# Low parts of 30 weights: from a VectorE subtraction to a ScalarE negative and an adding DMA

## The chip, the cores and the metric

One core of one Trainium2 chip runs the whole program. The metric is the device time of one execution in microseconds (us); lower is better. Engines are named as the profile names them: PE (matmuls), PEld (weight loads of PE), DVE (VectorE), ACT (ScalarE), POOL (GpSimd), SP (SyncE, which issues most transfers). Each engine runs its own instructions in order, and semaphores make it wait for others.

## What is computed

One layer over 1024 latent tokens of width 1024, with 256 context tokens:

```python
rgx, gate, s5u = split(modulate(x) @ w_in)        # three times 1024 columns
xc = centred_dwconv(rgx)                          # width 4
r, i = sigmoid(block_diag(xc)), sigmoid(...)      # 8 heads, both directions
h = linear_scan(exp(log_a), sqrt(-expm1(2 log_a)) * (i * xc))
rg = (h_fwd + h_bwd) * gelu(gate)
y = s5_fwd(s5u) + s5_bwd(s5u) + d * s5u           # complex diagonal states
s5 = gelu(y) * sigmoid(gelu(y) @ glu)
x = layer_norm(alpha * x + g1 * (concat(rg, s5) @ w_out))
x = layer_norm(alpha * x + g2 * sq_relu_mlp(modulate(x)))
```

Matmuls keep float32 accuracy by splitting both operands in a high part, rounded to the PE's fp32r format, and a low part, the rest: a product is wh·xh + wh·xl + wl·xh.

## The kernel before

**Weights.** `weights(src)` loads a 128x1024 block of a weight (512 KB) into a slot `wr` (three of them) by SP, and `split` makes two tiles of it: `wh`, a cast by ACT (line 98), and `wl = wr - wh`, a subtraction by DVE (`tt`, line 47). There are three slots each for `wh` and `wl`. `wr` is free when both have read it.

**Stages.** `project(m, ...)` multiplies one block of `w_in` with the tokens (line 380, products `ps_mm`). Its 24 blocks are eight for the RG-LRU input (`proj_rgx`, the first two of which take another way into the same sums), eight for the S5 input (`proj_s5`) and eight gates (`proj_gate`). While the S5 blocks and the S5 matrices are worked on, `rg_head` runs eight heads one after the other, each a chain: convolution on DVE, cast `xch` on ACT (line 421), gate products on PE (line 435, `ps_g`), sigmoids on ACT (line 437), after a table load exponentials (lines 442 and 443), after another the square root (line 446, tile `rr`), and then on DVE a step on `rr`, products and the linear scans (lines 455 to 458).

`s5_in` makes the S5 states' inputs H on PE and copies them out of PSUM (lines 603 to 606; for the second half all on ACT). `scan` runs 127 steps of three small DVE operations (tiles sT, sU, H) for each half of the groups; the two halves are interleaved. `proj_gate` evicts with a Gelu (line 636, tile `ge`) and multiplies by the RG-LRU's result on DVE.

The RG-LRU's half of the output projection has eight column blocks m. `mix_in(k)` loads the mixed rows k and splits them (tile `mh`): for k 0 to 4 the low part is a negative by ACT (line 664) and a DMA issued by POOL that adds the source from memory (line 665), for k 5 to 7 a subtraction by DVE. Columns 0 and 1 go together over all k (`k_outer`, line 694), columns 2 to 5 one by one (`prod`, line 675) through two PSUM banks with the tag "mm", columns 6 and 7 together again. `put_part` copies each bank out by ACT (line 681, tile `pt`).

`s5_states` copies the scanned states in the order in which the S5 output reads them (`h`, lines 724 and 725; for the first half both by ACT, 128 partitions in two halves), and `s5_out` multiplies them (lines 751 to 753, `ps_so`) and takes a Gelu (line 754, `gs`).

**Order.** The program is written stage by stage, but a list scheduler with its own estimates of durations and due times sets the order of each engine's queue. So an edit to one helper can move instructions far from it. A queue's order is fixed when the program is built.

Of the kernel before, what the change touches and what calls it, by code (L numbers as in the profile page):

```python
# [8 lines left out]
F32R = mybir.dt.float32r  # L9
I32 = mybir.dt.int32  # L10
AF = mybir.ActivationFunctionType
# [4 lines left out]
P = 128  # L16
# [25 lines left out]
def build(nc, tc, a, out):  # L42
    V, S, G, PE = nc.vector, nc.scalar, nc.gpsimd, nc.tensor
    MUL, ADD, SUB, MAX = ALU.mult, ALU.add, ALU.subtract, ALU.max

    def tt(o, x, y, op, eng=None):
        (eng or V).tensor_tensor(out=o, in0=x, in1=y, op=op)  # L47
# [10 lines left out]
    def ld(o, i):  # L58
        return nc.sync.dma_start(out=o, in_=i)

    def after(ins):
        return nullcontext() if ins is None else tc.issue_after(ins.ins)
# [4 lines left out]
    def f(t):  # L67
        return t.bitcast(F32)
# [3 lines left out]
    def pool(name, bufs=1, side="left", space=None, stack=es):  # L72
        kw = dict(name=name, bufs=bufs)
        if space is not None:
            kw["space"] = space
        else:
            kw["side"] = side
            kw["reuse_waits"] = "tile"
        return stack.enter_context(tc.tile_pool(**kw))
# [11 lines left out]
    wp = pool("wp")  # L91
# [3 lines left out]
    def split(raw, n, tag, hb, lb=None):  # L95
        hi = wp.tile([P, n], F32R, tag=tag + "h", name=tag + "h", bufs=hb)
        lo = wp.tile([P, n], F32R, tag=tag + "l", name=tag + "l", bufs=lb or hb)
        S.copy(hi, raw)  # L98
        tt(lo, raw, f(hi), SUB)
        return hi, lo  # L100
# [5 lines left out]
        S.activation(t, f(h), AF.Identity, bias=bias, scale=-1.0)  # L106
        stt(lo, x, scale, t, MUL, ADD)

    def weights(src, behind=None):
        raw = wp.tile([P, 1024], F32, tag="wr", name="wr", bufs=3)  # L110
        with after(behind):
            ld(raw, src)
        return split(raw, 1024, "w", 3)


    cols = con.tile([P, row(NCOLS)], F32, name="cols")
# [66 lines left out]
    def tmp(w=64, dt=F32):  # L183
        cnt[0] += 1
        return pp.tile([P, row(w)], dt, name=f"t{cnt[0]}")[:, 0:w]
# [25 lines left out]
    k = tmp()  # L211
# [85 lines left out]
    def fin_mod(mc, k, src):  # L297
        tt(mc, src, adab[:, :, k:k + 1].to_broadcast([P, 2, 2]), ADD)
        ts(mc[:, 1, :], mc[:, 1, :], 1.0, ADD)

    wrg = [weights(a["w_in"][m]) for m in range(2)]
    early = []
    for m in range(2):
# [3 lines left out]
    for k in range(KT):  # L307
# [18 lines left out]
        for r, src, pl_, n in ((0, xr, xlp, NL), (1, xc, xcp, NC)):  # L326
            h = pl_.tile([P, n], F32R, name=f"x{r}h{k}")
            lo = pl_.tile([P, n], F32R, name=f"x{r}l{k}")
            t = sup.tile([P, n], F32, tag=f"xt{r}", name="xt", bufs=1)
# [15 lines left out]
        for m in range(2):  # L345
            wh, wl = wrg[m]
# [20 lines left out]
    alt = [0]  # L367

    def project(m, ctx, evict, behind=None, load=None):
        wh, wl = weights(a["w_in"][m], load)  # L370
        src = [([x[:, s] for x in xh], [x[:, s] for x in xl], 512) for s in HS] + [(ch_, cl_, NC)]
        for i in (2, 0, 1) if ctx else (0, 1):
            hs, ls, n = src[i]
            alt[0] ^= ctx
            ps = psx.tile([P, n], F32, tag="si" if alt[0] and ctx else "mm", name="ps_mm", bufs=2)
            for k in range(KT):
                ks = slice(k * P, (k + 1) * P)
                with after(None if k else behind):
                    for c, (w, x) in enumerate(((wh, hs[k]), (wh, ls[k]), (wl, hs[k]))):
                        PE.matmul(ps, w[:, ks], x, start=(k == 0 and c == 0), stop=(k == KT - 1 and c == 2))  # L380
            evict(i, ps)
# [9 lines left out]
    def proj_rgx(m):  # L391
        xr = rp.tile([P, row(RGW)], F32, tag="rx", name="rx", bufs=2)
        for z in (slice(0, 1), slice(257, 260), slice(1284, 1286)):
            G.memset(xr[:, z], 0.0)

        def evict(i, ps):
            o, n = ((260, 512), (772, 512), (1, NC))[i]
            S.copy(xr[:, o:o + n], ps)

        if m < 2:  # L400
            for i, ps in enumerate(early[m]):
                evict(i, ps)
        else:
            project(m, True, evict)
        return xr
# [67 lines left out]
    def proj_s5(m):  # L473
        us = ev.tile([P, T8, NCH], F32, tag="us", name="us", bufs=1)

        def evict(i, ps):
            if i < 2:
                S.copy(us[:, :, CC + i::2], ps.rearrange("p (t c) -> p t c", t=T8))
            else:
                S.copy(us[:, :, 0:CC], ps.rearrange("p (c t) -> p t c", t=T8))  # L480

        project(16 + m, True, evict)
        d = dr.tile([T8, P, NCH], F32, name=f"u{m}")
        st_(d.rearrange("t p c -> p t c"), us)
        uscr[m] = d
# [184 lines left out]
    def prod(ps, w, x, js):  # L670
        (wh, wl), c = w, 0
        for k in range(KT):
            ks = slice(k * P, (k + 1) * P)
            for u, v in ((wh, x[k][:, 0]), (wh, x[k][:, 1]), (wl, x[k][:, 0])):
                PE.matmul(ps, u[:, ks], v[:, js], start=(c == 0), stop=(c == 3 * KT - 1))  # L675
                c += 1

    def put_part(m, pss):
        t = sc.tile([P, NL], F32, tag="gs", name="pt", bufs=2)
        for j, ps in enumerate(pss):  # L680
            S.copy(t[:, HS[j]], ps)
        part[m] = dr.tile([P, NL], F32, name=f"pt{m}")
        (G.dma_start if m > 5 else S.dma_start)(out=part[m], in_=t)

    def k_outer(ws, xs, tags, name, ks_=range(KT)):

        pss = [[psx.tile([P, 512], F32, tag=t, name=name, bufs=2) for j in range(2)] for t in tags]
        for i, k in enumerate(ks_):
            x = xs(k)
            ks = slice(k * P, (k + 1) * P)  # L690
            for (wh, wl), pp_ in zip(ws, pss):
                for j, ps in enumerate(pp_):
                    for c, (u, v) in enumerate(((wh, x[:, 0]), (wh, x[:, 1]), (wl, x[:, 0]))):
                        PE.matmul(ps, u[:, ks], v[:, HS[j]], start=(i == 0 and c == 0), stop=(i == KT - 1 and c == 2))
        return pss

    mix = []
# [2 lines left out]
        mix.append(mix_in(k))  # L700
        return mix[k]

    for m, pss in enumerate(k_outer([weights(a["w_out"][0, m]) for m in range(2)], mix_next, ("rg", "si"), "ps_wo")):
        put_part(m, pss)
    for m in range(2, 6):
        w = weights(a["w_out"][0, m])
        pss = []
        for j in range(2):
            pss.append(psx.tile([P, 512], F32, tag="mm", name="ps_wo", bufs=2))
            prod(pss[j], w, mix, HS[j])  # L710
        put_part(m, pss)
    for m, pss in enumerate(k_outer([weights(a["w_out"][0, m]) for m in (6, 7)], lambda k: mix[k], ("rg", "mm"), "ps_wo",
                                    (3, 4, 5, 6, 7, 0, 1, 2))):
        put_part(6 + m, pss)
    mixst.close()
# [87 lines left out]
    mxs, mix = {}, []  # L803
# [23 lines left out]
    for m in range(8):  # L827
        if m > 1:
            if m + 2 < 8:
                ahead.append(weights(a["glu"][m + 2]))  # L830
            w = ahead.pop(0)
# [148 lines left out]
    for j in range(2):  # L980
        ys = []
        for m in range(8):
            if 8 * j + m + 2 < 16:
                ahead.append(weights(a["w_out"][1, (m + 2) % 8]))
            w = ahead.pop(0)
# [86 lines left out]
    for p in range(0, NP1 + 4, 2):  # L1072
        if p < NP1:
            raw = wp.tile([P, 1024], F32, tag="wr", name="wr", bufs=3)
# [4 lines left out]
        wh, wl = w_ahead.pop(0)  # L1079
        for e in range(2):  # L1080
# [3 lines left out]
            t = ap_.tile([P, 512], F32, tag="r", name="p2", bufs=4)  # L1084
# [55 lines left out]
    def combo_next():  # L1140
        while len(c_ahead) < 4 and c_n[0] < len(stream):
            c = c_n[0]
            c_n[0] += 1
            if c % 2 == 0:
                c_tile[0] = [wp.tile([P, 1024], F32R, tag=t, name=t, bufs=3) for t in ("wh", "wl")]
            n, p = stream[c]
            src_ = operand(n, p)
            hi, lo = (x[:, HS[c % 2]] for x in c_tile[0])
            S.copy(hi, src_)  # L1149
            tt(lo, src_, f(hi), SUB)  # L1150
            c_ahead.append((hi, lo))
        return c_ahead.pop(0)

    XS = {"1": x0[0::2], "5": xt_[0], "6": xt_[1], "7": xt_[2], "3": x1, "4": xt_[3]}
    def rt():
        return ap_.tile([P, 512], F32, tag="r", name="r", bufs=4)
# [5 lines left out]
    for n, p in stream:  # L1162
        w = combo_next()
# [3 lines left out]
        if n == "1":  # L1167
# [3 lines left out]
            v, t = p2t.pop(p), rt()  # L1171
# [273 lines left out]
def program(arrays):  # L1445
    import concourse.bacc as bacc

    nc = bacc.Bacc("TRN2", target_bir_lowering=False, num_devices=1, dynamic_dma_scratch_size=1024)
    aps = {n: nc.dram_tensor(f"in_{n}", v.shape, mybir.dt.from_np(v.dtype), kind="ExternalInput").ap() for n, v in arrays.items()}
    out = nc.dram_tensor("out_0", (D, NL), F32, kind="ExternalOutput").ap()  # L1450
    with tile.TileContext(nc) as tc:
        build(nc, tc, aps, out)
    return nc
# [10 lines left out]
```

## Time and profile before

| | us |
|---|---|
| median of 3 runs | 1596.51 (1595.15 to 1600.73) |
| the profiled execution | 1594.69 |
| its span | 1592.9 |
| PE busy | 1476.7 (93%) |
| DVE busy | 1256.8 (79%) |
| ACT busy | 843.0 (53%) |
| POOL busy | 71.0 (4%) |
| mean granted clock of PE | 0.974 |

The span is what the trace covers. Busy shares are means over stages with different limits, so the table alone doesn't tell what an operation costs. A row of the timeline has the start, the duration, the engine, the line, the operation with output <- input, how many such stand in a row, and in brackets how long the engine had been idle and what ended that. Starts of pipelined instructions lie closer than their durations.

### The profile page before, as it was taken

How to read it: one execution, taken by the hardware profiler on the slowest of the kernel's cores; microseconds unless marked ns; L12 is line 12 of the kernel's file. 1: busy time of each engine (PE TensorE's matmuls, PEld its weight loads, DVE VectorE, ACT ScalarE, POOL GpSimd, SP SyncE). 2: the span in 40 equal slices, each digit the busy share in tenths (PEclk: the TensorE clock that was granted, in tenths of full speed). 3: DMA queues.
4: the chain of work that ended last, by engine and by line, in shares of the span. 5: the costliest groups of instructions: out<-in, count | busy, mean ns of one | idle time of the engine just before them, and what ended most of it. 6: DMA issues, size and time to landing. Idle time of an engine off the chain costs nothing. (4 is left out here: it accounts for less than half of the span.)

```text
span 1592.9 us, 20440 instructions
## 1 busy us (share of the span) xinstructions
PE 1476.7 (93%) x7148; PEld 1202.4 (75%) x7148; DVE 1256.8 (79%) x2555; ACT 843.0 (53%) x1178; POOL 71.0 (4%) x141
## 2 busy tenths in 40 slices
PE   7899998999978999699999799989899899999997
PEld 2687777778756878598878677867788788888886
DVE  7899999998866989635978789778787566667877
ACT  4675656666795331954233576444555554344425
POOL 0000000000000000000000011111111000000000
PEclk9999999999999999799999999999999999999999
DMA  7623323323664752983768576777764786776703
GB/s 255 233 94 119 115 99 120 105 106 119 231 215 137 209 183 91 264 201 119 228 207 265 173 242 232 279 248 268 245 219 167 268 287 215 263 251 210 240 7 106
DMA packets 131382, 304.16 MB, mean 191 GB/s; under 512 B 16208, under 2 KB 47440, under 8 KB 129872
## 3 DMA queue, kind: packets, MB, share of 16 engines
q1 hardware_dynamic: 104048, 237.45, 46.9%
q0 software_dynamic: 13184, 47.72, 8.4%
q10 hardware_dynamic: 14048, 17.70, 3.1%
q8 instruction: 56, 0.92, 0.2%
q14 instruction: 46, 0.38, 0.1%
HBM read 219.52 MB, written 83.30 MB: 190 GB/s over the span
## 5 line engine op out<-in xcount | busy, mean ns | idle before, releaser
L98 ACT CAST wh<-wr 128x1024 fp32r<-128x1024 f32 x113 | 118.4, 1051 | 230.0 <-PE ps_m L1276 73.8
L47 DVE TENSOR_TENSOR wl<-wr,wh 128x1024 fp32r<-128x1024 f32 (+1 forms) x161 | 170.5, 1060 | 83.7 <-ACT wh L98 77.2
L1066 PE MATMUL ps_m<-xt,wh 128*128 128x512 f32 x512 | 160.7, 395 | 0.0
L1276 PE MATMUL ps_m<-bh,wh 128*128 128x512 f32 x392 | 153.7, 392 | 3.8 <-ACT bh L1238 3.7
L1276 PE MATMUL ps_m<-bl,wh 128*128 128x512 f32 x392 | 153.4, 391 | 0.5 <-DVE bl L47 0.5
L1276 PE MATMUL ps_m<-bh,wl 128*128 128x512 f32 x392 | 153.3, 391 | 0.0
L380 PE MATMUL ps_mm<-x0h,wh 128*128 128x512 f32 x352 | 140.3, 399 | 1.0 <-ACT wh L98 1.0
L380 PE MATMUL ps_mm<-x0h,wl 128*128 128x512 f32 x352 | 140.0, 399 | 0.9 <-DVE wl L47 0.9
L380 PE MATMUL ps_mm<-x0l,wh 128*128 128x512 f32 x352 | 140.0, 398 | 0.0
L1066 PEld LDWEIGHTS ps_m<-xt,wh 128*128 128x128 f32 x512 | 97.5, 191 | 21.2 <-issue 0.3
L1066 PE MATMUL ps_m<-xt,wl 128*128 128x512 f32 x256 | 101.9, 398 | 10.5 <-DVE wl L47 10.5
L1276 PEld LDWEIGHTS ps_m<-bh,wh 128*128 128x128 f32 x392 | 73.8, 188 | 20.6 <-ACT bh L1238 4.1
L1276 PEld LDWEIGHTS ps_m<-bl,wh 128*128 128x128 f32 x392 | 74.0, 189 | 16.6 <-DVE bl L47 1.0
L1276 PEld LDWEIGHTS ps_m<-bh,wl 128*128 128x128 f32 x392 | 74.0, 189 | 15.5
L675 PE MATMUL ps_wo<-ms,wh 128*128 128x512 f32 x256 | 81.7, 400 | 2.7 <-ACT ms L799 2.7
L1066 PE MATMUL ps_m<-x,wh 128*128 128x512 f32 x256 | 81.8, 400 | 1.0 <-ACT wh L1149 1.0
L380 PEld LDWEIGHTS ps_mm<-x0h,wl 128*128 128x128 f32 x352 | 67.2, 191 | 14.3 <-DVE wl L47 1.4
L380 PEld LDWEIGHTS ps_mm<-x0h,wh 128*128 128x128 f32 x352 | 67.1, 191 | 13.5 <-ACT wh L98 1.4
L380 PEld LDWEIGHTS ps_mm<-x0l,wh 128*128 128x128 f32 x352 | 67.1, 191 | 12.5
L47 DVE TENSOR_TENSOR sT<-al,H 128x128 f32<-128x128 f32 x254 | 66.9, 286 | 1.3
L1066 PEld LDWEIGHTS ps_m<-xt,wl 128*128 128x128 f32 x256 | 49.0, 191 | 23.6 <-DVE wl L47 13.4
L47 DVE TENSOR_TENSOR bl<-br,bh 128x1024 fp32r<-128x1024 f32 x49 | 59.5, 1218 | 2.2 <-ACT bh L1238 2.2
(352 smaller groups left out, 3696.2 us busy)
## 6 DMA issues: line engine op xcount, KB each, us to landing
wr<-in_w SPq DMA_DIRECT2D x79, 512.0 KB, 5.2
br<-hq SPq DMA_DIRECT2D x49, 512.0 KB, 5.0
mo<-in_ada_t SPq DMA_DIRECT2D x32, 512.0 KB, 4.1
hq<-hs POOLq DMA_DIRECT2D x14, 1024.0 KB, 8.2
wr<-in_w_in SPq DMA_DIRECT2D x24, 512.0 KB, 4.3
wr<-in_w_out SPq DMA_DIRECT2D x24, 512.0 KB, 4.5
xt<-xt ACTq DMA_DIRECT2D x16, 512.0 KB, 2.7
yd<-Y SPq DMA_DIRECT2D x16, 512.0 KB, 2.6
```

Of the source, the lines that this page charges most:

```text
L47: (eng or V).tensor_tensor(out=o, in0=x, in1=y, op=op)
L98: S.copy(hi, raw)
L380: PE.matmul(ps, w[:, ks], x, start=(k == 0 and c == 0), stop=(k == KT - 1 and c == 2))
L675: PE.matmul(ps, u[:, ks], v[:, js], start=(c == 0), stop=(c == 3 * KT - 1))
L1066: PE.matmul(ps, u[:, ks], v, start=(first and c == 0), stop=(last and c == 11))
L1276: PE.matmul(pss[m], w[:, 512 * k + P * m:512 * k + P * m + P], x[:, 512 * k:512 * k + 512], start=(q == 0 and k == 0 and c == 0), stop=(q ...
```

## The change

`weights` gets a second way, used for all `project` blocks (22; the first two RG-LRU blocks keep theirs) and for the eight blocks of the RG-LRU's half of `w_out`: the low part is written by ACT as the negative of the high part, and a DMA that POOL issues adds the block from memory once more. Loads, products and tile counts stay. The other weights (S5's half of `w_out`, GLU, MLP) keep DVE's subtraction.

```diff
-    def weights(src, behind=None):
+    def weights(src, behind=None, add=False):
         raw = wp.tile([P, 1024], F32, tag="wr", name="wr", bufs=3)
         with after(behind):
             ld(raw, src)
-        return split(raw, 1024, "w", 3)
+        if not add:
+            return split(raw, 1024, "w", 3)
+
+        hi, lo = (wp.tile([P, 1024], F32R, tag=t, name=t, bufs=3) for t in ("wh", "wl"))
+        S.copy(hi, raw)
+        S.activation(lo, f(hi), AF.Copy, scale=-1.0)
+        G.dma_start(out=lo, in_=src, accum_op=ADD)
+        return hi, lo
...
     def project(m, ctx, evict, behind=None, load=None):
-        wh, wl = weights(a["w_in"][m], load)
+        wh, wl = weights(a["w_in"][m], load, add=True)
...
-    for m, pss in enumerate(k_outer([weights(a["w_out"][0, m]) for m in range(2)], mix_next, ("rg", "si"), "ps_wo")):
+    for m, pss in enumerate(k_outer([weights(a["w_out"][0, m], add=True) for m in range(2)], mix_next, ("rg", "si"), "ps_wo")):
...
     for m in range(2, 6):
-        w = weights(a["w_out"][0, m])
+        w = weights(a["w_out"][0, m], add=True)
...
-    for m, pss in enumerate(k_outer([weights(a["w_out"][0, m]) for m in (6, 7)], lambda k: mix[k], ("rg", "mm"), "ps_wo",
+    for m, pss in enumerate(k_outer([weights(a["w_out"][0, m], add=True) for m in (6, 7)], lambda k: mix[k], ("rg", "mm"), "ps_wo",
```

The lines of `weights` shift all later lines by 7. The scheduler also orders the queues anew. Two places of ACT's queue show it. The first is where the last copy of the S5 inputs (H) is done and the gates go on; `ge` is a gate's Gelu, `wh` and `wl` are the parts of gate and output weights. Before:

```order
L606 COPY H_3775<-ps_si 64x2x128
L636 ACTIVATE ge<-ps_mm 128x512
L98 CAST wh<-wr 128x1024 x3
L636 ACTIVATE ge<-ps_mm 128x512 x2
L98 CAST wh<-wr 128x1024
L636 ACTIVATE ge<-ps_mm 128x512 x2
```

After:

```order
L613 COPY H_3789<-ps_si 64x2x128
L643 ACTIVATE ge<-ps_mm 128x512
L117 CAST wh<-wr 128x1024 x2
L118 ACTIVATE wl<-wh 128x1024 x2
L643 ACTIVATE ge<-ps_mm 128x512
L117 CAST wh<-wr 128x1024
L118 ACTIVATE wl<-wh 128x1024
```

Two casts are followed by two negatives where three casts stood, and the first adding DMA of this group can be issued only behind the first of those negatives.

The second place is on ACT again, where the copies of the scanned states (`h`, of the first half of H) begin; `pt` is the eviction of an output column block. Before, the last evictions of columns 4 and 5 stand ahead of all copies:

```order
L681 COPY pt<-ps_wo 128x512
L98 CAST wh<-wr 128x1024
L681 COPY pt<-ps_wo 128x512
L724 COPY h_5982<-H_3774 64x1024
L683 DMA pt_5167<-pt 128x1024
L725 COPY h_5982<-H_3774 64x1024
```

After, the rows from the last eviction of column 3 on:

```order
L688 COPY pt<-ps_wo 128x512
L118 ACTIVATE wl<-wh 128x1024
L690 DMA pt_5071<-pt 128x1024
L731 COPY h_6012<-H_3788 64x1024
L688 COPY pt<-ps_wo 128x512
L732 COPY h_6012<-H_3788 64x1024
L731 COPY h_6012<-H_3788 64x1024
L732 COPY h_6012<-H_3788 64x1024
L731 COPY h_6017<-H_3788 64x1024
L732 COPY h_6017<-H_3788 64x1024
L688 COPY pt<-ps_wo 128x512
L117 CAST wh<-wr 128x1024
```

Here the first copy stands ahead of column 4's first eviction, and five more ahead of its second; column 5's evictions follow behind further copies in the same way.

## Rows read from the trace of the kernel before

**Rows 1.** Busy us (instructions) by 40 us: PE, PEld, DVE, ACT, POOL, PEclk, DMA, GB/s.

```profile
320.00:360.00 40.00, 37.62 (x211) 31.43 (x210) 39.82 (x55) 27.81 (x40) 0.00 (x0) 1.00 0.28 104
...
440.00:480.00 40.00, 28.88 (x147) 22.05 (x145) 26.19 (x82) 38.25 (x80) 0.00 (x0) 0.96 0.63 215
...
520.00:560.00 40.00, 40.00 (x178) 33.10 (x178) 38.74 (x207) 13.16 (x16) 2.59 (x3) 1.00 0.76 216
...
600.00:640.00 40.00, 40.00 (x176) 32.77 (x175) 39.79 (x226) 9.21 (x11) 0.00 (x0) 1.00 0.26 84
640.00:680.00 40.00, 25.15 (x136) 22.27 (x135) 23.72 (x76) 38.81 (x27) 1.13 (x2) 0.79 0.99 247
```

**Rows 2.** Timeline of ACT over one head: start, us, instruction [idle before, releaser].

```profile
342.99 1.26 ACT L421 CAST xch<-xc 128x1283 fp32r<-128x1283 f32 x1 [2.62 <-DVE xc L56]
...
359.15 1.28 ACT L442 ACT_TABLE_LOAD   x1
...
366.89 2.43 ACT L446 ACTIVATE rr<-rr 128x1280 f32<-128x1280 f32 x2
...
385.33 1.26 ACT L421 CAST xch<-xc 128x1283 fp32r<-128x1283 f32 x1 [2.97 <-DVE xc L56]
```

**Rows 3.** Timeline of DVE behind that square root.

```profile
368.54 2.89 DVE L56 SCALAR_TENSOR_TENSOR rr<-aa,rr 128x1280 f32<-128x1280 f32 x2
```

**Rows 4.** PE's waits, 60 to 400 us: total, times, longest.

```profile
PE ps_g L435 <- ACT xch L421: 13.8, 6, 3.0
```

**Rows 5.** Groups by shape, 60 to 680 us: count, busy us, mean ns.

```profile
L47 DVE TENSOR_TENSOR wl<-wr,wh 128x1024 fp32r<-128x1024 f32 x33 | 40.0, 1217 | 12.4 <-ACT wh L98 12.4
...
L724 ACT COPY h<-H 64x1024 f32<-64x1024 f32 x10 | 20.0, 1998 | 6.3 <-DVE H L47 6.2
```

**Rows 6.** Tile mh (min/median/max ns, first and last start); the page's transfer xt.

```profile
L694 PE MATMUL ps_wo<-mh,wl x64: 387/389/397, 560.4 to 651.2; 128*128 128x512 f32 x64
...
L664 ACT ACTIVATE mh<-mh x5: 1047/1061/1062, 535.2 to 563.6; 128x1024 fp32r<-128x1024 f32 x5
L665 POOL DMA_DIRECT2D mh<-mx x5: 842/856/885, 536.5 to 565.0; - x5
L47 DVE TENSOR_TENSOR mh<-mraw,mh x3: 1216/1225/1225, 569.1 to 576.8; 128x1024 fp32r<-128x1024 f32 x3
...
DMA to landing us min/median/max: 5.9/7.6/9.4
...
xt<-xt ACTq DMA_DIRECT2D x16, 512.0 KB, 2.7
```

**Rows 7.** Timeline of ACT behind the S5 inputs' copies.

```profile
492.23 2.93 ACT L98 CAST wh<-wr 128x1024 fp32r<-128x1024 f32 x3
```

**Rows 8.** Timeline of PE there, with the first products of gate 2.

```profile
493.32 0.50 PE L380 MATMUL ps_mm<-x0h,wh 128*128 128x512 f32 x1 [0.98 <-ACT wh L98]
...
494.99 0.50 PE L380 MATMUL ps_mm<-x0h,wl 128*128 128x512 f32 x1 [0.93 <-DVE wl L47]
...
495.55 0.39 PE L380 MATMUL ps_mm<-x0l,wh 128*128 128x512 f32 x1
495.78 0.40 PE L380 MATMUL ps_mm<-x0h,wl 128*128 128x512 f32 x1
```

**Rows 9.** Timeline of DVE before the first scan's end: three operations of the interleaved scans.

```profile
635.26 0.29 DVE L47 TENSOR_TENSOR sT<-al,H 128x128 f32<-128x128 f32 x1
...
635.73 0.30 DVE L47 TENSOR_TENSOR sT<-al,H 128x128 f32<-128x128 f32 x1
```

**Rows 10.** Timeline of ACT around the state copies.

```profile
630.36 0.58 ACT L681 COPY pt<-ps_wo 128x512 f32<-128x512 f32 x1
637.14 2.08 ACT L724 COPY h<-H 64x1024 f32<-64x1024 f32 x1 [6.20 <-DVE H L47]
...
673.21 1.08 ACT L754 ACTIVATE gs<-ps_so 128x512 f32<-128x512 f32 x2
```

**Rows 11.** Timeline of PE behind that Gelu.

```profile
673.86 0.80 PE L751 MATMUL ps_so<-mt,u 128*128 128x128 f32 x2 [13.01 <-ACT gs L754]
```

## Prediction made before the change was run

> **What bounds the kernel now.** I read the page's busy shares first, then the busy time by stretches of 40 us, then what each engine waited for, and last the instructions one by one where a wait stood. The change touches only work between 70 and 640 us, and four stages lie there, each with another limit [rows 1]. From 80 to 420 (the RG-LRU heads) PE is busy 37.6 of 40 us in the row shown, DVE 39.8, ACT 27.8: two engines look full. From 420 to 491 ACT is full (38.3 of 40) with copies of the S5 states. From 491 to 651 PE is full (40.0 in both rows) and DVE nearly so (38.7 and 39.8). From 637 to 673 ACT is full (38.8) and PE sits at 25.2. Behind 680 PE is full again and the order is the same in both kernels.
>
> A full DVE is not yet a bound, so I followed one head. Its cast on ACT begins at 342.99, the gates' sigmoids end where the exponentials' table load begins, 359.15, the square root follows at 366.89, and the next head's cast comes at 385.33 [rows 2]. On DVE the first thing behind the root begins at 368.54 [rows 3], that is 0.4 us after the first of the two roots is through (366.89 + 2.43 / 2 = 368.1). So DVE came to that place almost as soon as its operand did. From there to the next cast it is 16.8 us of the head's own DVE chain, with no low part of a weight in it. The same gap in the eight heads adds to about 4.4 us; that is all that a lighter DVE can give here. PE's largest wait in this stretch is for that cast, 13.8 us in six waits [rows 4]: PE waits for the chain.
>
> **Part 1, DVE is relieved.** 30 low parts at 1.217 us each [rows 5] go, about 1.14 us apiece by the spacing of starts, 34 us in all: 16 up to the tail of the head stage, 14 behind 491. In the head stage this is filler between chain links, so it gives at most 4.4 us.
>
> **Part 2, ACT and POOL get work.** 30 negatives at 1.06 us, 30 DMA issues at 0.86 us, and a landing 5.9 to 9.4 us after the issue, 7.6 in the middle; all three are rows of the one construct of this kind that the kernel has, the low part of the mixed tile [rows 6]. The quickest transfer of this size on the page, without an addition, lands in 2.7 us [rows 6]: that is the lower bound. POOL is idle, ACT has some 12 us in 40 free in the head stage [rows 1]. So a low part comes about 1.06 + 0.3 + 7.6 = 9 us after its cast, where DVE took some 1.2 us. For most weights the order leaves 10 to 40 us between the negative and the first product that reads it; there the transfer is hidden.
>
> **Head stage.** The new order puts 12.8 us more products ahead of the end of the last head's gates on PE (350.1 us of work for 337.3), which had some 22 us of waits there, and negatives among the sigmoids: the work from first gate product to last, each instruction in the order taken at its mean in the trace, sums to 105.5 us over the heads where it was 101.8, +3.7. Against at most −4.4 from DVE, of which I take half: about +1.5 us, bounds −4 (all of the gaps gone, nothing lost) and +8 (PE does not fit the extra work into its waits).
>
> **Gate 2, behind the S5 copies.** Until 492.2 ACT is full. Before, its three casts follow (492.23), DVE makes the low part, and PE waits 0.98 and 0.93 us; its first low-part product begins at 494.99 [rows 7, 8]. Now: two casts to 494.2, negative to 495.2, issue 0.3, landing 7.6: 503.1. PE stands at the third product of gate 2 and can do nothing else in its order: 8.1 us later than before (6.4 to 9.9 with the ends of those five landings, 3.2 with the bound of 2.7). I take the five rows in the middle: they are the same operation. The other weights of this stage have 10 us or more and cost nothing. Here the page of the Trainium skill, DMA: Bandwidth & Descriptors, Anatomy of one DMA — SWDGE (gpsimd) path, says otherwise: about 2.0 us and bytes by 436e3, an estimate of 3.2 us for 512 KB, by which this stall would be 4.4 us shorter. The rows of the adding DMA say 7.6 for that size, in a stretch where the DMA engines were 0.76 busy [rows 1].
>
> **The first scan on DVE.** DVE loses that stall too, but has 1.3 us less to do between the gate products, so that its last low part of a mixed tile (before: begins at 576.8, ends at 578.0 [rows 6]) ends at about 584.8. Behind it stood 331 scan operations and six low parts before the first scan's end at 637.1; in the new order 259 operations stand there and no low part, because scan steps filled the gaps earlier. Two interleaved scans take 0.47 us per three operations (635.26 to 635.73 [rows 9]), so 259 take 40.8: the first scan ends at about 625.6, 11.5 us earlier (621 if DVE follows PE more closely, 627.5 with a late landing).
>
> **The state copies on ACT, where I see the loss.** A copy of a state takes 2.0 us [rows 5]; 12 of them (24 us) run from 637.14 on, 16 in all until the first Gelu of the S5 outputs at 673.21, for which PE waited 13.0 us [rows 10, 11]. Before, they sat behind all evictions of output columns 2 to 5 (the last at 630.36), so PE ran on undisturbed to its last product of this half at 651.3 [rows 6]. In the new order these copies come earlier, and the evictions of columns 4 and 5, two casts and a negative sit among them. PE has two banks for these columns, so it must wait for each eviction. Laying the new order out from 625.6: one copy, eviction (628.2); five copies, eviction (638.9, PE waits 5.3); cast, negative, two copies, eviction (645.6); four copies, cast, eviction (655.2), and only then PE gets the second bank of columns 6 and 7 and has 87 products left at 0.23 us [rows 8]: 655.2 + 19.9 = 675.1, where it was 651.3. Behind this end (E) come the last evictions, a cast, four copies (8 us), a cast and the Gelu: PE's next S5 product at E + 11.1 = 686.2 instead of 673.86 [rows 11]: +12.3 us. With 621 it is +7.7, with 627.5 +14.2. The 13 us that PE waited before are not saved; they become waits in the middle of its products. Products that come behind a wait may also run at a lower granted clock: 0.79 in the stretch that holds the 13 us wait, 1.00 in the one ahead of it [rows 1]. I add 1 for it.
>
> **Sum.** +1.5 + 12.3 + 1 = +14.8 us. The profiled execution took 1594.7 us (span 1592.9), 1.8 us under the median of the runs, 1596.5. So 1609.5 there, 1611 in terms of the median; I say 1610. Its own range: −4 + 7.7 = +3.7 up to +8 + 14.2 + 3 = +25, of which I take the middle, 1602 to 1619, since the ends would have to come together.
>
> **Rivals.**
> *DVE was the bound (faster).* DVE is full in both PE-bound stages, and what it gives up is 34 us. If PE's and ACT's waits in the head stage really hang on DVE's queue, the heads win up to 8 us; and if the first scan ends at 621 and the evictions keep ahead of the copies, the copies start 16 us earlier and the 13 us wait goes. Then −10 to −20, 1577 to 1587. For it: DVE at 39.8 of 40 [rows 1]. Against it: the gap of 0.4 us in the chain [rows 2, 3], and the order of ACT's queue, which puts copies ahead of evictions. It needs the first scan to end only after PE has handed over the columns 4 and 5, or PE's other banks to cover it. Chance 0.14.
> *The two cancel (within 0.3%).* The first scan ends at 621 and the heads win their 4 us: +7.7 − 4 = +3.7, 1600. For it: ACT had room among the sigmoids before. Against it: the heads' sum above. Chance 0.15.
> *The adding DMA lands as quickly as a plain one.* At 2.7 us gate 2 resumes some 5 us earlier than I forecast, the first scan ends at 621, and the loss at the end is 7.7: with 1.5 and 1 it is +10, 1607. For it: the transfers at gate 2 run in a quieter stretch than the five measured ones. Against it: the least of the five is 5.9 [rows 6]. Chance 0.05. The rate of the page of the Trainium skill named above would put the time here.
> *PE is the bound of the heads as well (slower still).* The 12.8 us of products do not fit the waits, +8 in the heads, and the lower clock costs 3: 1596.5 + 8 + 12.3 + 3 = 1620. Chance 0.13.
> *My forecast*, 1602 to 1619: 0.53.
> *That the work isn't moved at all* is excluded: the new order has 30 low parts less on DVE.
>
> **How the numbers follow.** A measurement of this kernel tells about 0.3% (4.8 us) from no change. The range reaches from 1596, which cuts off the faster rival and a little of the cancelling one, to 1621. Faster 0.14 (the first rival); same 0.15 (the second); slower 0.71 (the rest).
>
> **What would show it.** PE's wait for a low part at gate 2, 7 to 10 us where two waits of 1 stood; the landing of the added DMAs, 6 to 9 us. The first state copy at 621 to 628 instead of 637.14. PE waits for evictions of columns 4 to 7 between 625 and 660, 13 us or more in sum, with ACT full of state copies; the last product of this half near 675; PE's first S5 product near 686. The cast of the last head within 8 us of 385.33. I am wrong if the evictions' waits stay under 5 us, if the landing takes 3, or if the last head's cast comes more than 5 us earlier.

## Result and profile after

| | before | changed |
|---|---|---|
| median, us | 1597.18 (1595.15 to 1600.73, 4 runs) | 1638.22 (1635.81 to 1640.25, 4 runs) |
| ratio, 95% interval | 1 | 1.0257 (1.0235 to 1.0278) |
| span of the profiled execution, us | 1592.9 | 1638.2 |
| mean granted clock of PE | 0.974 | 0.960 |

The change costs 41 us, where +14 was forecast, and the time lies outside the range (1596 to 1621). The same places in both traces show where the execution falls behind; each time is a start, and each difference contains the ones above it.

| place | before | changed | later by |
|---|---|---|---|
| DVE's step behind the last head's root | 409.00 | 424.07 | 15.1 |
| last copy of the S5 inputs (ACT) | 491.08 | 505.62 | 14.5 |
| first low-part product of gate 2 (PE) | 494.99 | 517.85 | 22.9 |
| last low part of a mixed tile by DVE | 576.81 | 614.02 | 37.2 |
| first state copy (ACT) | 637.14 | 656.10 | 19.0 |
| last product of this half (PE) | 651.20 | 707.73 | 56.5 |
| first S5 product behind the Gelu (PE) | 673.86 | 718.74 | 44.9 |
| end of the span | 1592.9 | 1638.2 | 45.3 |

Everything is lost between 60 and 720 us. The stages of the changed kernel, which answer to [rows 1] (busy us by stretches; PE, PEld, DVE, ACT, POOL, then granted clock, share of the DMA engines, GB/s):

```profile
320.00:360.00 40.00, 37.63 (x213) 31.99 (x212) 36.13 (x49) 28.36 (x35) 2.59 (x3) 1.00 0.51 144
...
560.00:600.00 40.00, 35.16 (x146) 28.41 (x145) 27.67 (x161) 15.07 (x19) 4.34 (x5) 0.91 0.82 212
600.00:640.00 40.00, 31.76 (x132) 25.36 (x131) 34.82 (x200) 15.91 (x19) 5.19 (x6) 0.91 0.84 218
640.00:680.00 40.00, 33.03 (x134) 25.93 (x132) 33.57 (x173) 26.75 (x19) 1.75 (x2) 0.91 0.44 107
680.00:720.00 40.00, 29.25 (x141) 24.73 (x142) 4.69 (x5) 19.02 (x18) 1.11 (x2) 0.89 0.73 183
```

DVE is relieved as intended (36.1 of 40 us where [rows 1] had 39.8 in the same stretch), and PE, which was busy 40.0 of 40 from 600 to 640, has 31.8 at a granted clock of 0.91. The DMA engines are busy 0.84 there, where they were 0.26; but by 600 us the kernel before had the mixed tiles behind it. Over the same stage, from the first cast of a mixed tile to the start of the last low part of one (before, then changed), they are equally busy, and the stage is longer:

```profile
534.00:577.00 43.00, 40.26 (x176) 32.47 (x175) 37.05 (x192) 17.85 (x21) 4.30 (x5) 1.00 0.84 235
```

```profile
560.00:614.00 54.00, 40.99 (x164) 32.81 (x163) 36.51 (x200) 19.93 (x23) 6.06 (x7) 0.87 0.83 217
```

One head of the changed kernel on ACT, the seventh as in [rows 2]:

```profile
355.08 1.26 ACT L428 CAST xch<-xc 128x1283 fp32r<-128x1283 f32 x1 [1.52 <-DVE xc L56]
...
373.27 1.28 ACT L449 ACT_TABLE_LOAD   x1
...
381.01 2.44 ACT L453 ACTIVATE rr<-rr 128x1280 f32<-128x1280 f32 x2
...
399.82 1.26 ACT L428 CAST xch<-xc 128x1283 fp32r<-128x1283 f32 x1 [3.27 <-DVE xc L56]
```

From the cast to the table load it is 18.2 us where it was 16.2; from there to the root 7.74 in both; from the root to the next cast 18.8, before 18.4. So the gate phase grew, and DVE's part did not shrink.

What PE waited for behind the heads (timeline of PE; idle time and what ended it in brackets), from gate 2 to the S5 outputs; the second answers to the second wait of [rows 8], the last to [rows 11]:

```profile
511.19 0.80 PE L387 MATMUL ps_mm<-x0h,wh 128*128 128x512 f32 x1 [2.60 <-ACT ge L643]
517.85 0.79 PE L387 MATMUL ps_mm<-x0h,wl 128*128 128x512 f32 x1 [5.43 <-DMA wl<-in_w_in]
573.58 0.80 PE L387 MATMUL ps_mm<-x0h,wh 128*128 128x512 f32 x1 [4.84 <-ACT ge L643]
609.01 0.79 PE L701 MATMUL ps_wo<-mh,wh 128*128 128x512 f32 x1 [8.17 <-DMA mh<-mx]
658.64 0.73 PE L682 MATMUL ps_wo<-mh,wh 128*128 128x512 f32 x2 [1.09 <-ACT pt L688]
669.34 1.22 PE L682 MATMUL ps_wo<-mh,wh 128*128 128x512 f32 x2 [4.91 <-ACT pt L688]
685.50 1.22 PE L701 MATMUL ps_wo<-mh,wh 128*128 128x512 f32 x2 [6.46 <-ACT pt L688]
718.74 0.80 PE L758 MATMUL ps_so<-mt,u 128*128 128x128 f32 x2 [5.25 <-ACT gs L761]
```

Three of them were not in the forecast: 2.60 us at gate 2 for a Gelu, which stands behind two casts and two negatives in ACT's new queue, 4.84 us for another Gelu, and 8.17 us for the transfer of a mixed tile. ACT's timeline has the reason of the second: in the new order two casts of mixed tiles stand ahead of that Gelu (572.94) where one stood, and the later one waits 8.48 us for its load. What PE loses there hangs on when the load lands: in `copies_late` (below), with the same order up to there, the cast waits 5.07 us and PE not at all. DVE's timeline has a product that waits for a load of the RG-LRU's result:

```profile
571.04 1.04 ACT L669 CAST mh<-mraw 128x1024 fp32r<-128x1024 f32 x1 [8.48 <-DMA mraw<-mx]
...
572.94 0.59 ACT L643 ACTIVATE ge<-ps_mm 128x512 f32<-128x512 f32 x1
```

```profile
588.97 0.69 DVE L47 TENSOR_TENSOR ge<-ge 128x512 f32<-128x512 f32 x1 [4.18 <-DMA ge<-hs]
```

Behind each of the long waits PE ran for a while at the lower of its two clock levels (1.2 GHz), here behind gate 2's:

```profile
518.44 0.63 PE L387 MATMUL ps_mm<-x0h,wh 128*128 128x512 f32 x1
518.86 0.63 PE L387 MATMUL ps_mm<-x0l,wh 128*128 128x512 f32 x1
...
524.36 0.40 PE L387 MATMUL ps_mm<-x0l,wh 128*128 128x512 f32 x1
524.60 0.39 PE L387 MATMUL ps_mm<-x0h,wl 128*128 128x512 f32 x1
```

The starts lie 0.42 us apart at first and 0.24 later. Between 490 and 720 us the changed kernel has 43 such slow pairs of neighbouring products of 512 columns, the kernel before none. At 0.2 us each that is some 8 us of PE's time, an estimate.

The adding DMAs land as forecast (7.6 in the middle was taken; gate 2's own, issued at 510.11, took 7.7), but those of the mixed tiles, which had 7.6 [rows 6], now share the engines with them. First the 30 added ones, then the mixed tiles' five:

```profile
DMA to landing us min/median/max: 5.3/7.0/11.1
...
DMA to landing us min/median/max: 5.2/10.4/11.6
```

### The profile page after: what moved, and what is told of

The parts are those of the page before. It is cut to its first block, busy times and chain, and to the rows that moved or that the text cites. A ratio compares the mean times of both kernels' runs of the same rounds, so it can differ in the third digit from the quotient of the medians.

```text
span 1638.2 us, 20490 instructions
## 1 busy us (share of the span) xinstructions
PE 1491.7 (91%) x7148; PEld 1213.4 (74%) x7148; DVE 1227.2 (75%) x2525; ACT 871.8 (53%) x1208; POOL 96.9 (6%) x171
## 5 line engine op out<-in xcount | busy, mean ns | idle before, releaser
L47 DVE TENSOR_TENSOR wl<-wr,wh 128x1024 fp32r<-128x1024 f32 (+1 forms) x131 | 134.3, 1025 | 100.8 <-ACT wh L98 85.8
L98 ACT CAST wh<-wr 128x1024 fp32r<-128x1024 f32 x83 | 87.1, 1050 | 181.4 <-PE ps_m L1283 75.2
L608 PE MATMUL ps_si<-ub,xt 128*128 128x160 f32 x256 | 47.9, 329 | 25.5 <-ACT H L613 14.3
L608 PEld LDWEIGHTS ps_si<-ub,xt 128*128 128x128 f32 x256 | 39.2, 203 | 35.2 <-ACT H L613 22.0
```

The source lines that it names most:

```text
L608: last_in[m] = PE.matmul(ps[:, i, :], xt[:, g, i, :], ub[:, 4 * q + g, :], start=True, stop=True)
```

## Experiments

Three questions: is the loss in the places that the forecast named; is it the work or the new order of the queues; and whose queue.

**One part alone.** The flag `add` is set for some blocks only:

```diff
-        wh, wl = weights(a["w_in"][m], load, add=True)
+        wh, wl = weights(a["w_in"][m], load, add=not 8 <= m < 16)
```

This is heads_only; gates_only has `add=8 <= m < 16`, and both leave the output projection to DVE. In wout_only `project` has no `add` and the eight blocks of the output projection keep it.

> Only the 14 blocks of the head stage (6 RG-LRU inputs, 8 S5 inputs) take the negative and the adding DMA; gates and output projection keep DVE's subtraction. Before 1597, changed kernel 1638. Theory by places: the trace of the changed kernel is 15 us late at the end of the head stage, so 1607 to 1613, with the state copies behind the evictions as before and PE's 13 us wait still there. Theory by number (each adding DMA costs the same, 41 us / 30 = 1.4 us): 1597 + 14 x 1.4 = 1616. Theory by interaction (the head stage alone is harmless, its lateness comes from the other parts): 1593 to 1599.

> Only the eight gate blocks change. Theory by places: the wait at gate 2 (8 us), and whatever of the 14 us between gate 2 and the end of the mixed tiles belongs to the gates, partly given back since the first scan needs less of DVE: 1602 to 1615. Theory by number: 1597 + 8 x 1.4 = 1608. These two differ in the trace: by places the wait stands at gate 2 in one piece.

> Only the eight blocks of the output projection change. In its order two state copies stand ahead of column 4's second eviction and five ahead of each of column 5's. Theory by places (evictions behind copies): 1605 to 1618, with PE waiting for evictions 10 us or more. Theory by number: 1608. If the copies' place is harmless: 1595 to 1600.

Measured: the head stage alone 1.0101 (1.0064 to 1.0138), the gates alone 1.0131 (1.0097 to 1.0166), the output projection alone 1.0054 (1.0035 to 1.0073). In medians that is 1611.8, 1616.0 and 1604.1: the first inside what was expected, the second 1 us above it, the third 1 us below it. Each part loses by itself, so the rival of an interaction falls, and a fixed price per DMA isn't seen either (1.1, 2.6 and 1.1 us for each). The three add up to 2.9%, the whole change costs 2.6%, but this doesn't show that the parts are independent, since each run has a queue order of its own. With the gates' blocks PE waits 5.26 us for gate 2's transfer at 504.54, and also 9.19 us for an eviction at 662.17; with the output projection's 8.55 us for an eviction at 650.97, and also 8.94 us for a mixed tile at 580.10:

```profile
504.54 0.79 PE L387 MATMUL ps_mm<-x0h,wl 128*128 128x512 f32 x1 [5.26 <-DMA wl<-in_w_in]
```

```profile
650.97 1.22 PE L701 MATMUL ps_wo<-mh,wh 128*128 128x512 f32 x2 [8.55 <-ACT pt L688]
```

**The relief alone.**

```diff
-        hi, lo = (wp.tile([P, 1024], F32R, tag=t, name=t, bufs=3) for t in ("wh", "wl"))
+        hi = wp.tile([P, 1024], F32R, tag="wh", name="wh", bufs=3)
         S.copy(hi, raw)
-        S.activation(lo, f(hi), AF.Copy, scale=-1.0)
-        G.dma_start(out=lo, in_=src, accum_op=ADD)
-        return hi, lo
+        return hi, hi
```

> The 30 subtractions are left out and nothing takes their place (the third product reads the high part, so the low part of these 30 weights is missing from the result). It is what DVE's relief alone is worth, with an order of its own (four copies ahead of column 4's last eviction). My theory: DVE is no bound in the head stage (at most 4 us) and the copies ahead of evictions take back what the earlier scan gives: 1590 to 1603. Rival, DVE is the bound: 1565 to 1582.

Measured 1.0077 (1.0046 to 1.0108): 30 subtractions less and nothing in their place is slower. I had expected 1590 to 1603; it was 1609, and the trace shows the heads 11 us late (DVE behind the last root at 419.98, before 409.00) with no work added that could delay them. The only difference left there, besides the work taken off, is the order of the queues, which the scheduler wrote anew.

**Two places of the order put back.** `heads_hold` is heads_only with gate 0 queued on PE behind the last head's gate products; `copies_late` queues the state copies behind the last eviction of column 5 (`after` orders a queue and waits for nothing; `table_g[0]` is the last gate product traced, `last_pt[5]` column 5's last eviction):

```diff
-        project(8 + m, False, evict, last_in[m] if m else None, in_ld[m - 2] if m >= 2 else None)
+        project(8 + m, False, evict, last_in[m] if m else table_g[0], in_ld[m - 2] if m >= 2 else None)
...
-        S.copy(h2[0:64], src[0:64, :, :, CC - 1:NCH - 1])
+        with after(last_pt[5]):
+            S.copy(h2[0:64], src[0:64, :, :, CC - 1:NCH - 1])
...
```

> As the run with the head stage's blocks alone (1612), but the first product of gate 0 is queued on PE behind the last gate product of head 7, where it stood before the change: 38 of the 57 products of 512 columns that the new order had moved ahead of the heads' end go back behind it. Theory (the heads are longer because PE was given that work inside the chain, and not because of the transfers or ACT's negatives): 38 x 0.23 = 8.7 us come back, 1601 to 1606, and the last head's root about 413 to 415 instead of 422. Rival (latency and contention of the adding DMAs): no change, 1608 to 1616.

> The changed kernel with the state copies of the first half queued on ACT behind the last eviction of column 5, nothing else. Theory (evictions behind copies cost): PE's three waits for evictions (12.5 us) go, copies begin near 669 and not at 656, the first Gelu of the S5 outputs comes about 11 us earlier: 1638 - 11 = 1627 (1622 to 1632). Rival (the wait only moves from the evictions to the copies): 1635 to 1641.

> The run without the 30 subtractions (their low part missing from the result, 1609) with both places of the order put back: gate 0 behind the heads, state copies behind column 5's evictions. Theory (what made the relief a loss is the order at these two places): 8.7 us from the heads, some 10 from the copies: 1586 to 1594, that is a gain of 3 to 11 us over the kernel before. Rival (the relief is worthless or harmful in itself): 1600 to 1610.

> The changed kernel with the two places of the order put back and gate 2's low part left to DVE. Theory by places: 1638 - 8.7 (heads) - 11 (copies) - 7 (gate 2) = 1611 (1604 to 1618), the rest being the mixed tiles' late loads and the crowded transfers between 560 and 640. Rival (adding DMAs cost by their number, whatever the order): above 1625.

`copies_late` did what was expected: 1625.7, ratio 1.0176 (1.0135 to 1.0216), 12.5 us below the changed kernel; the three waits for evictions are gone, and the Gelu's wait is 8.42 us. `heads_hold` gave nothing: 1.0105 (1.0072 to 1.0138), as heads_only. Its trace says why it is no proof against PE's order. Of the 13.3 us that the last root of heads_only is late (422.28 for 409.00), 11.7 are lost before the last head's cast (397.00 for 385.33), where the hold changes nothing. In the last head itself PE, without gate 0's products, stands idle and then runs slowly, and the gate phase (first to last gate product) takes 14.7 us where it took 13.8:

```profile
400.46 1.01 PE L442 MATMUL ps_g<-xch,gwh 128*128 128x256 f32 x2 [4.33 <-ACT xch L428]
404.11 0.58 PE L442 MATMUL ps_g<-xcl,gwh 128*128 128x256 f32 x1 [2.65 <-DVE xcl L47]
...
408.50 0.63 PE L442 MATMUL ps_g<-xcl,gwh 128*128 128x512 f32 x1
408.92 0.63 PE L442 MATMUL ps_g<-xch,gwl 128*128 128x512 f32 x1
...
414.43 0.39 PE L442 MATMUL ps_g<-xch,gwl 128*128 128x512 f32 x1
414.66 0.39 PE L442 MATMUL ps_g<-xch,gwh 128*128 128x512 f32 x1
```

At 408.5 two products of 512 columns start 0.42 us apart, at 414.4 0.23 us: after 4.33 and 2.65 us of waiting the clock was at 1.2 GHz, later at 2.4 (mean granted clock of 400 to 440: 0.84, in heads_only 0.87). `relief_hold_late` came out at 0.9994 (0.9972 to 1.0017), 1599.5 where 1586 to 1594 was expected, and `all_ordered` at 1.0152 (1.0114 to 1.019): the copies' place counts, gate 0's does not, and the sum by places, which expected 1611 for the last, misses 12 us. Part of this miss is gate 2: with its low part back on DVE its first low-part product begins 7.0 us earlier than in copies_late (508.82 for 515.84), but the first S5 product only 3.5 us earlier (697.78 for 701.30), and the medians differ by 2.7 us.

**The whole order put back.** So the question was put once for all: the same work in the order of the kernel before, instruction by instruction on every engine, by edges between neighbours in a queue that order and wait for nothing. What is new (negatives, DMAs) is put in between by the scheduler, at the same places of ACT's queue in all runs that have the 30 negatives. The kernel before was not itself run with such edges, so that they cost nothing is not shown. In the diff `order` is a queue of the kernel before, each instruction by its place in the program's text.

```diff
+        for x, y in zip(order, order[1:]):
+            tc.add_manual_dep(seen[e][y], seen[e][x].name, how, reason="pin")
```

> First step of a ladder in which every engine keeps the order of the kernel before, instruction by instruction (edges that order the queues and wait for nothing). Here the 30 subtractions are left out and nothing takes their place (low part of these weights missing). In its own order this run took 1609. Theory (that loss was the order alone): no slower than before; the heads win at most 4 us, the first scan ends earlier and the copies move up to the last eviction, some 6 us: 1586 to 1594. Rival (taking work off DVE costs in itself, for instance by a lower clock on PE): 1603 to 1612.

> Second step: with ACT's 30 negatives, without the DMA (the low part is only the negative, so the result lacks the addition). Order as before on every engine, the negatives where the third step has them. Theory: ACT has room nearly everywhere; among the sigmoids and behind the S5 copies a negative delays others by about 1 us each: 2 to 6 us over the first step, 1588 to 1600. Rival (ACT is the bound): 10 us or more over the first step.

> Third step: the whole changed kernel in the order of the kernel before, on every engine; only the negatives and the added DMAs are put in. In its own order it took 1638. Theory (most of the 41 us is the order): the wait at gate 2 stays (8 us) and the crowded transfers around the mixed tiles cost up to 8: 1598 to 1612. Rival (the work itself costs it): 1625 to 1640.

> As the third step, but the 30 DMAs write the block plainly and add nothing (the result is then not the low part). It tells what the addition costs: a plain transfer of 512 KB lands in 2.7 to 5 us, the adding one in 7.0 by the median of the changed kernel's trace. Theory (the landing sets the wait at gate 2): 2 to 4 us less there than in the third step, and less crowding behind: 4 to 8 us below the third step. Rival (the addition is free, only the bytes count): equal to the third step.

| order of the kernel before, and | ratio (95%) | last root, DVE |
|---|---|---|
| 30 subtractions left out | 0.9950 (0.9926 to 0.9975) | 407.70 |
| and 30 negatives | 0.9983 (0.9964 to 1.0002) | 414.36 |
| and 30 adding DMAs (all of the change) | 1.0087 (1.0056 to 1.0118) | 412.46 |
| the DMAs write plainly, without adding | 1.0072 (1.0046 to 1.0098) | 412.41 |
| for comparison: all of the change, own order | 1.0257 (1.0235 to 1.0278) | 424.07 |

This divides the loss. DVE's relief is worth 0.5%, some 8 us, and where this run's text put it: the copies begin at 631.59, right behind column 5's last eviction at 631.11. ACT's negatives cost 0.3% by the middle values (the intervals overlap), nearly all in the heads by the trace (5.3 us more from first to last gate product, summed over the heads). The DMAs cost 1.0%, some 17 us: PE's wait at gate 2 grows from 1.17 us (negatives alone) to 11.23, its wait for a mixed tile from 4.50 to 9.32:

```profile
508.62 0.79 PE L387 MATMUL ps_mm<-x0h,wl 128*128 128x512 f32 x1 [11.23 <-DMA wl<-in_w_in]
...
595.43 0.79 PE L701 MATMUL ps_wo<-mh,wh 128*128 128x512 f32 x1 [9.32 <-DMA mh<-mx]
```

The stage of the mixed tiles grows with them: from the first cast to the last it is 43.4 us with negatives alone, 44.9 with plain writes, 50.7 with the addition. The new order costs the rest, 1.0257 − 1.0087 = 1.7%, some 27 us (22 by the medians, which come from two sets of runs): the largest part of the loss isn't work at all. With plain writes the same two waits are 7.75 and 2.15 us and the landing 4.9 in the middle (6.7 with the addition), but the intervals of the two ratios overlap; how much of the 17 us is the addition and how much the bytes stays open.

**Whose queue.** Two runs put back one engine's order alone, and one asks whether the construct pays where the transfers have room:

> The changed kernel with PE's order alone put back to that of the kernel before; ACT, DVE, SP and POOL keep the new one. All orders together gave back 22 us (1638 to 1616). Theory (the heads' part of it is PE's filling work between the gate products, the rest is ACT's queue): the last head's root 8 to 12 us earlier, 1626 to 1631, and the waits for evictions stay. Rival (PE's order is irrelevant, as the run that held back gate 0 might say): 1634 to 1641.

> The changed kernel with ACT's order alone put back (negatives where the run with all orders had them). Theory: the state copies stand behind the evictions again, worth 12 us as in the run that moved only these, and the casts of the mixed tiles stand behind the gates' Gelus, up to 4 more: 1621 to 1627. If ACT's order also carries the heads: 1615 to 1620. Rival (no effect): 1634 to 1641.

> Only columns 2 to 7 of the output projection take the negative and the adding DMA, in the order of the kernel before: their weights are loaded behind the mixed tiles, their products begin 10 us or more later, and ACT and the transfers are idle there. Theory: six subtractions (6.9 us) leave DVE behind the last mixed tile, the first scan ends up to 6.9 us earlier, the copies start at the last eviction: 4 to 6 us faster than before, a ratio of 0.996 to 0.9975. Rival (the transfers still crowd the mixed tiles' or delay a product): 1.000 to 1.004.

PE's order alone: 1630.9, ratio 1.0222 (1.0199 to 1.0245), the last root at 415.11 instead of 424.07. ACT's alone: 1630.9, ratio 1.0211 (1.0189 to 1.0232), no waits for evictions, but the heads longer still (last root 427.09, the gate phases 121.4 us in sum where the changed kernel has 114.2): ACT's old order doesn't fit PE's new one. Each gives back some 7 us (the first at the short end of what was expected, the second 4 us short of it), 14 together; all orders at once give 22 us by the medians and 27 by the ratios. So some 7 to 9 us of the heads is PE's order by the traces (415.11 against 424.07, or against the 422.39 of copies_late, whose heads have the changed kernel's order), 12.5 us is the place of the copies in ACT's queue (copies_late), and the rest, up to 5 us, I can't put down to one engine.

Where PE's order costs can be seen in the fifth and the sixth head. Both kernels have 36 gate products in each. How many other products stand between the first and the last of them, and how long that takes:

| | fifth head | sixth head |
|---|---|---|
| before | 8, 12.2 us | 19, 12.1 us |
| changed | 28, 14.1 us | 42, 15.7 us |
| changed, PE's order put back | 8, 12.6 us | 19, 12.7 us |
| 30 subtractions left out, own order | 28, 14.3 us | 40, 15.8 us |
| 30 negatives, all orders as before | 8, 14.6 us | 19, 13.4 us |

With more products in between the phase is longer, with ACT's negatives or without them; the last row shows that negatives alone can also lengthen these two.

Columns 2 to 7 alone in the old order: 0.999 (0.9967 to 1.0013), no difference that can be told. Its trace has the gain that was expected, the first copy at 631.81 instead of 637.14 and the S5 product at 668.94 instead of 673.86, but the times don't bear it out. No version here that does the whole computation beats the kernel before.

## Why the prediction was wrong

**Right.** That DVE is no bound in the heads: with the old order its relief moved the last root from 409.00 to 407.70, 1.3 us where at most 4.4 was forecast. Gate 2: 8.1 us forecast; from the last S5 copy to its first low-part product the changed kernel takes 8.3 us more (22.9 − 14.5), and its own landing was 7.7 where 7.6 was taken. (What this wait is worth at the end is less, 3 us or so by `all_ordered`.) The scan: 40.8 us forecast behind the last mixed tile, 40.9 measured (615.2 to 656.10). The rate of the Trainium skill's page DMA: Bandwidth & Descriptors, Anatomy of one DMA — SWDGE (gpsimd) path, gives an estimate of 3.2 us for this size; no adding DMA of this trace landed under 5.2, and even the plain ones of plain_pinned took 4.9 in the middle, so the measurement decides. The evictions behind the state copies: copies_late gives 12.5 us back. From the first state copy to the first S5 product the changed kernel loses 25.9 us (44.9 − 19.0) where 23.8 was forecast (12.3 + 11.5).

**Where the sum fails.** At the first S5 product it had +13.8 us (1.5 + 12.3), measured +44.9. Of the 31 us between, 13.6 are lost in the heads, some 15 between gate 2 and the last mixed tile, and 2 behind the first state copy.

**Wrong, first step: the head stage, +1.5 us, measured +15.1.** The forecast summed the work of a gate phase by mean durations and set half of DVE's 4.4 us against it. The trace shows the phases from first to last gate product 6.2 us longer in sum (114.2 for 108.0, where the forecast had +3.7), 2.4 us more from the cast to the first gate product, in the first, fourth and seventh head, where the new order puts a transposition ahead of it on PE (with the negatives in the old order this part is unchanged), 2.5 from the sigmoids to the step on DVE, where the forecast had −2.2, and 4.1 ahead of the first cast (2.5 in copies_late, with the same queues up to there, so part of it is scatter of one execution). By the ladder 3.5 of the 15.1 us is work (412.46 for 409.00 with everything in the old order; the negatives alone give 6.7 and the relief −1.3) and 11.6 is order (424.07 for 412.46). The rival that PE's extra products do not fit the waits had 8 us for this and a chance of 0.13. It was the right side; it was rated low because I took PE's idle time as room. The idle time lies ahead of a gate phase ([rows 4]: the waits are for its cast), and the products stood inside it: 5.6 of the 6.2 us are in the fifth and sixth head of the table above, where PE isn't idle at all between the first and the last gate product.

**Wrong, second step: nothing between gate 2 and the mixed tiles.** The sum took "The other weights of this stage have 10 us or more and cost nothing", and had the last mixed tile 6.8 us late. It was 37.2 late, 14.3 of it lost between these two places. The added transfers do hide, each for itself, apart from gate 2's, but they share the DMA engines with what PE, ACT and DVE wait for there. In the kernel before these engines were already 0.84 busy in the stage of the mixed tiles; the software queue's transfers took 33.5% of them for 43 us then, 40.4% for 54 us now, 14 and 22 us, and the stage got 11 us longer. (Measured with the order held, adding DMAs make it 7.3 us longer, 43.4 to 50.7.) The new order has also put one more cast that waits for such a load ahead of a Gelu. That an adding DMA takes twice the engines' time per byte could have been seen ahead of the change: the kernel before has five of them, and in its stretch of 560 to 600 us the software queue took 14.5% of the engines for 1.05 MB, the first hardware queue 35.7% for 4.98 MB:

```profile
q1 hardware_dynamic: 1584, 4.98, 35.7%
q0 software_dynamic: 288, 1.05, 14.5%
```

**What followed from it: the first scan 11.5 us earlier.** It needed the second step to be right. The scan took its time as forecast, but began 37 us late, so its end came 19.0 us later, and the copies' collision with the evictions came on top of that.

**Too small: the lower clock, +1.** It stood for the products behind one wait. The changed kernel has five waits of 4.8 us or more between gate 2 and the end of this half, and the slow products behind them take some 8 us longer; this is contained in the places above.

**The range.** 1621 is the sum of the upper ends (8 for the heads, 14.2 for the scan and the copies, 3 for the clock), and has none for crowded transfers. A cost "hidden" by slack in the order needed an upper end too.

## What to carry to other kernels

What an engine's relief is worth is read from the chain that waits for it: 34 us of work taken off a VectorE that looked full gave 8. Where a scheduler writes the queues, a change has two prices, its work and the order that comes with it, and they can be told apart by running the new work in the old order; here the order was the dearer one (1.7% of 2.6%). A transfer that is hidden by its own slack still delays those that are not: sum the DMA engines' time in the stretch before calling it free.

## What the runs showed of the hardware

An adding DMA from memory took the DMA engines twice the time of a plain one of the same bytes. The software queue in the same stretch (600 to 640 us) of the two runs with the whole change in the old order, first with the addition, then with plain writes (packets, MB, share of the 16 engines):

```profile
q0 software_dynamic: 638, 2.35, 33.9%
```

```profile
q0 software_dynamic: 720, 2.62, 18.9%
```

That is 14.4% of the engines' time per MB and 7.2%. The second thing is PE's clock after a wait. In heads_hold, taking fill work out of the last head gave no time back there: the products behind the waits of 4.33 and 2.65 us started at the lower of the two levels. In the changed kernel the same is seen behind each of the five long waits.
